# Expert layer of a diffusion trunk: rounds of a fixed mix in its first half, and small experts' rows collected by transfers inside SBUF

## The chip, the cores and the metric

One core of a Trainium2 chip runs the whole forward pass in one launch. The metric is the device time of that launch in microseconds; less is better. The arithmetic is f32, with matmuls either in f32 or as three f32r products of a high and a low part.

## The reference, cut to what matters

A trunk of two layers over 256 latent tokens and 256 context tokens, D = 1024. The first layer's channel mixer is dense. The second one's is a top-2-of-8 expert SwiGLU on the 256 latent tokens, with D_FF_EXPERT = 3584; it is the part that the change touches.

```python
def moe_swiglu(t, router, wg, wu, wd):
    logits = (t @ router).astype(jnp.float32)
    top_val, top_idx = lax.top_k(logits, TOP_K)
    top_w = jax.nn.softmax(top_val, axis=-1)
    gates = jnp.sum(jax.nn.one_hot(top_idx, N_EXPERTS, dtype=jnp.float32) * top_w[..., None],
                    axis=1).astype(t.dtype)
    out = jnp.zeros_like(t)
    for e in range(N_EXPERTS):
        out = out + gates[:, e:e + 1] * swiglu(t, wg[e], wu[e], wd[e])
    return out
```

Each expert needs its three weight matrices, 8 x 3 x 1024 x 3584 x 4 bytes = 352 MB in all, each byte once.

## The kernel before, in words

Everything up to the router runs first. The router then ranks the experts by their number of tokens (rank r = 0 is the fullest; "expert r" below means the expert of rank r) and gives each rank a fixed capacity (CAPS). Tokens are gathered into slots. A slot group of 128 tokens is a "B" unit, of 64 an "A", of 32 a "C". Rank 0 has a B and an A; rank 1 a B and a C; ranks 2 and 3 three C each, as a pair and a single; ranks 4, 5 and 6 an A each; rank 7 one C.

Each expert is worked through in 84 *steps*; a step uses one block of weights of 512 KB (a `raw` tile, 4 KB a partition). 56 steps are for the two up matrices (`up`, in four groups by columns, the last of them 512 wide instead of 1024), 28 for the down matrix (`down`). A B unit's step is `dense`: ACT and VectorE split the block into a high and a low part (`split_w`, L1159 and L1160), and PE runs three f32r matmuls for each product (`mm3`, L243 to L245). A and C units take the block as it is, in f32 (`few`, `mm_few`, L1281), with the tokens packed: a C unit's block is cut into four column pieces that run side by side in four 32-column strips of PE, so its result lies in four groups of 32 partitions, each for a quarter of the columns (an A unit: two groups of 64).

The steps are put into *rounds* by hand. `drive` runs a round thus: the dense matmuls of the round before, the packed ones of this round, then the splits for the next round are handed to ACT and VectorE, then the loads of blocks up to RAW = 16 ahead, then what has come due (`due`, filled by `after(n, ...)`: transposes of hidden values, scatters). PE's order is exactly this order (`manual_schedule`); the other engines' orders are set by the framework's scheduler. SP issues all weight loads, in step order; each waits until its buffer of the ring `raws` is free. The lists are made by `beside` (two steps of the main stream and a share of the others in each round; the last 32 steps alone, four a round). Main are ranks 1, then 0. The others are `weave(whole(7), whole(2) + whole(3))`, which alternates between whole groups (16, 8 or 28 steps) of rank 7 and of ranks 2 and 3, and then ranks 4, 5 and 6. That makes 92 rounds of 7 or 8 steps (4 at the end); rank 1 is main in rounds 0 to 41, rank 0 in 42 to 83. In the first 42 rounds lie 320 of the 672 steps.

When an expert's last step is done, `take` (L1421, L1422) copies the result from PSUM as a high and a low part (`yB`, `yA`, `yC`). `finish` calls `places`: for each slot group POOL copies its part of the placement matrix `pick` side by side to full width (`pd`, L1437, one buffer) and PE transposes it (L1441). In the rounds after, `scatter` (L1470) multiplies the placement with the result, 256 columns at a time where there is a C unit (four rounds, two token tiles each), 512 otherwise; for a C or A unit these are matmuls on 32 or 64 rows, one pair for each slot group. VectorE adds them, times the gate, to `acc` (L1474). The last finished expert (rank 6) takes a way of its own (`fin`, `Final`).

PSUM of the layer: three banks "b" for experts with a B unit, three "a" for the others, two "q" for transposes and scatters.

Of the kernel before, what the change touches and what calls it, by code (L numbers as in the profile page):

```python
# [11 lines left out]
F32R = mybir.dt.float32r  # L12
# [6 lines left out]
D = 1024  # L19
# [26 lines left out]
WIDE = {"B": 128, "A": 64, "C": 32}  # L46


RAW = 16

UPS = [(0, 1024), (1024, 1024), (2048, 1024), (3072, 512)]

# [2 lines left out]
def trunk(ctx: ExitStack, tc: tile.TileContext, I, out, dbg=None):  # L55
    nc = tc.nc
    V, S, G, PE = nc.vector, nc.scalar, nc.gpsimd, nc.tensor
# [36 lines left out]
    def chain(*gens):  # L94
        for g in gens:
            yield from g

    def fr(ap):
        return ap.bitcast(F32)
# [9 lines left out]
    identr = kq.tile([128, 128], F32R, name="identr")  # L109
# [321 lines left out]
    def evac(dst, src):  # L431
        evac_n[0] += 1
        if evac_n[0] % 2:
            S.activation(dst, src, AF.Copy)
        else:
            V.tensor_copy(dst, src)
# [523 lines left out]
    for i in range(DEPTH):  # L960
        last = i == DEPTH - 1
        n = 1 if last else 2
        u = new_u()
# [5 lines left out]
        with ExitStack() as mx:  # L969
            def pools(name):  # L970
                return mx.enter_context(tc.tile_pool(name=f"{name}{i}", bufs=1))

            y = mixer(i, u, n, pools, begun if i == 0 else None, ((filters(), 18),) if i == 0 else (),
                      () if last else ((ada_cols(i, 3), AP + 1),
                                       (chain(ada_cols(i, 4, R_GF), ada_part(i, 2)), 2 * AP + 1)))
# [11 lines left out]
        if not last:  # L987
            u = new_u()
# [16 lines left out]
    i = DEPTH - 1  # L1005
    u = new_u()
# [10 lines left out]
    with tc.tile_pool(name="route", bufs=1) as rp:  # L1017
# [105 lines left out]
        pick = mr.tile([128, 2, 768], F32R, name="pick")  # L1123
        for c0, r, b, kind in COLS:
            w = WIDE[kind]
# [14 lines left out]
    pm = ctx.enter_context(ExitStack())  # L1140
    rawp = pm.enter_context(tc.tile_pool(name="raws", bufs=RAW))
    mp = pm.enter_context(tc.tile_pool(name="moe", bufs=1))
    mps = pm.enter_context(tc.tile_pool(name="mps", bufs=4, space=PSUM))

    def mbank(tag, dt=F32):

        return mps.tile([128, 512], dt, name="m" + tag, tag=tag, bufs={"b": 3, "a": 3, "q": 2}[tag])
# [26 lines left out]
    units = {r: [] for r in range(NE)}  # L1174
    for c0, r, _, kind in COLS:
        u = units[r]
# [12 lines left out]
    def after(n, fn, *args):  # L1189
        due.setdefault(now[0] + n, []).append((fn, args))  # L1190

    def drive(rounds):
        flat = [(n, s) for n, rnd in enumerate(rounds) for s in rnd]
        raws, tiles, ahead = {}, {}, [0, 0]

        def load(upto):
            while ahead[0] < min(upto, len(flat)):
                raws[ahead[0]] = load_raw(flat[ahead[0]][1][1](), *flat[ahead[0]][1][2])
                ahead[0] += 1

        def split(rnd):
            while ahead[1] < len(flat) and flat[ahead[1]][0] <= rnd:
                s = flat[ahead[1]][1]
                load(ahead[1] + 1)
                raw = raws.pop(ahead[1])
                tiles[ahead[1]] = (raw,) + (split_w(raw, *s[2]) if s[3] else ())
                ahead[1] += 1

        load(RAW)
        first_tokens()  # L1210
        split(0)
        n = 0
        with tc.manual_schedule(engines={mybir.EngineType.PE}):
            old = []
            for r, rnd in enumerate(rounds):
                for s, t in old:
                    s[3](t)
                old = [(s, tiles[n + i]) for i, s in enumerate(rnd) if s[3]]
                for i, s in enumerate(rnd):
                    if s[4]:  # L1220
                        s[4](tiles[n + i])
                    tiles.pop(n + i)
                n += len(rnd)
                split(r + 1)
                load(n + RAW)
                for fn, args in due.pop(now[0], []):
                    fn(*args)
                now[0] += 1
                if r == len(rounds) - 3:
                    places(rnd[-1][0])  # L1230
                    fin.append(Final())
            while due:
                now[0] = min(due)
                for fn, args in due.pop(now[0]):
                    fn(*args)

    def beside(main, others, tail):

        out, j, n = [], 0, len(main) // 2
        for i in range(n):  # L1240
            upto = (i + 1) * (len(others) - tail) // n
            out.append(main[2 * i:2 * i + 2] + others[j:upto])
            j = upto
        while j < len(others):
            out.append(others[j:j + 4])
            j += 4
        return out

    def weave(*streams):

        out, done = [], [0] * len(streams)
        total = [sum(map(len, g)) * (1 if i else 0.8) for i, g in enumerate(streams)]
        while any(streams):
            j = min((done[j] / total[j], j) for j in range(len(streams)) if streams[j])[1]
            g = streams[j].pop(0)
            done[j] += len(g)
            out += g
        return out

    def gather(c0, n, dst):  # L1260

# [146 lines left out]
    ys = {}  # L1408

    def take(u, o):  # L1410

        ys[u] = []
        n = min(512, 8 * WIDE[u[0]] * (len(u) - 1))
        for ob in o:
            tag = "big" if u[0] == "B" else "yA" if n == 512 else "yC"
            y = mp.tile([128, 2, n], F32R, name="y" + u[0], tag=tag, bufs=1 if tag == "yA" else 2)
            src = ob[:, 0:n]
            if fin:
                src = mp.tile([128, n], F32, name="yg", tag="sgA", bufs=3)
                V.tensor_mul(src, ob[:, 0:n], fin[0].gy)  # L1420
            S.activation(y[:, 0], src, AF.Copy)  # L1421
            V.tensor_sub(y[:, 1], src, fr(y[:, 0]))  # L1422
            ys[u].append(y)

    pts = {}

    def places(r):

        for u in units[r]:
            w = WIDE[u[0]]  # L1430
            for j, c0 in enumerate(u[1:]):
                if u[0] == "B":
                    pds = [pick[:, t, c0:c0 + 128] for t in range(2)]
                else:
                    g = 128 // w
                    pd = mp.tile([128, 2, g, w], F32R, name="pd", tag="pt")
                    G.tensor_copy(pd, fr(pick[:, :, None, c0:c0 + w]).to_broadcast([128, 2, g, w]))  # L1437
                    pds = [pd[:, t].rearrange("p a s -> p (a s)") for t in range(2)]
                q = mbank("q", F32R)
                for t in range(2):  # L1440
                    PE.transpose(q[:, 128 * t:128 * t + 128], pds[t], identr)  # L1441
                p = mp.tile([128, 2, 128], F32R, name="pt" + u[0], tag="ptF", bufs=6)
                evac(p, fr(q[:, 0:256]).rearrange("p (t s) -> p t s", s=128))
                pts[u, j] = p

    def finish(r):
        if not fin:
            places(r)
        n = 256 if any(u[0] == "C" for u in units[r]) else 512
        cells = [(c0, t) for c0 in range(0, D, n) for t in range(2)]  # L1450
        for j, (c0, t) in enumerate(sorted(cells, key=lambda x: x[1]) if fin else cells):
            after(1 + j // 2, scatter, r, t, c0, n)

    fin = []

    def scatter(r, t, c0, n):
        o = mbank("q")[:, 0:n]
        ops = []
        for u in units[r]:
            w = WIDE[u[0]]  # L1460
            for j in range(len(u) - 1):
                for a in range(2):
                    if u[0] == "B":
                        ops.append((pts[u, j][:, t], ys[u][c0 // 512][:, a, c0 % 512:c0 % 512 + n]))
                    else:
                        q, i = divmod(c0, 8 * w)
                        i += 8 * w * j
                        ops.append((pts[u, j][w * q:w * q + w, t], ys[u][0][w * q:w * q + w, a, i:i + n]))
        for j, (l, m) in enumerate(ops):
            PE.matmul(o, l, m, start=(j == 0), stop=(j == len(ops) - 1))  # L1470
        sl = acc[0][:, t, c0:c0 + n]
        g = gates_r[:, t, r:r + 1]
        if not fin:
            V.scalar_tensor_tensor(sl, o, g, sl, op0=OP.mult, op1=OP.add)  # L1474
        else:
            with tc.issue_after(newest[0].ins):
                sl = fin[0].o[t][:, c0:c0 + n]
                V.scalar_tensor_tensor(sl, o, g, sl, op0=OP.mult, op1=OP.add)
                fin[0].add(t, c0 // 512)

    def whole(r):

        return [g for fb in range(len(UPS)) for g in up(r, fb)] + down(r)

    def flat(groups):
        return [s for g in groups for s in g]
# [33 lines left out]
    def first_tokens():  # L1520
# [5 lines left out]
        for r in range(NE):  # L1526
            for u in units[r]:
# [2 lines left out]
        acc.append(hp.tile([128, 2, D], F32, name="acc", tag="H1"))  # L1530
        G.memset(acc[0], 0.0)

    drive(beside(flat(whole(1) + whole(0)), weave(whole(7), whole(2) + whole(3)) + flat(whole(4) + whole(5) + whole(6)),
                 32))


    flag = nc.values_load(ctli[0:1, 8:9], min_val=0, max_val=NE)
# [128 lines left out]
```

## Time and profile before

| | us |
|---|---|
| runs of the kernel before (median of 3) | 1880.66 |
| their lowest and highest | 1878.2, 1880.77 |
| the profiled execution: its time | 1878.78 |
| the profiled execution: its span | 1877.0 |

The profiled execution is one of the kind of the three; its span is the time from the first to the last instruction. The expert layer's rounds begin at 943.6 us; the last scatter of the layer ends at 1864.6. The engines: PE = TensorE's matmuls, PEld its weight loads, DVE = VectorE, ACT = ScalarE, POOL = GpSimd, SP = SyncE, which issues the weight loads. Ends of matmuls are modelled, so that starts are the better measure of pace: a row's pitch is the distance between two starts. f32 matmuls and their weights are two instructions each. PEclk is the granted clock of TensorE as a share of its full 2.4 GHz; in a short stretch a mean between 0.5 and 1 is a part of it at the lower level.

### The profile page before, as it was taken

The page shows a single profiled execution, that of the slowest core. Times are in us where ns is not written, and L with a number is a line of the kernel's source. Part 1 is how long each engine was busy: PE and PEld are TensorE (multiplying, and loading weights), DVE is VectorE, ACT ScalarE, POOL GpSimd, SP SyncE. Part 2 cuts the span into 40 slices and gives each one's busy share as a digit, 9 for nine tenths or more (in the row PEclk, how much of TensorE's full clock was granted, in tenths as well). Part 3 has the DMA queues.
Part 4 walks back from the last instruction along what each step waited for, and adds up shares of the span by engine and source line. Part 5 has one row for each costly group of instructions (what it writes and reads, how often), then busy time and mean ns, then how long its engine had stood idle before and what let it go on. Part 6 is the DMA issues. An engine that isn't in the chain of part 4 may idle for free.

```text
span 1877.0 us, 34065 instructions
## 1 busy us (share of the span) xinstructions
PE 1792.9 (96%) x13502; PEld 1221.3 (65%) x13502; DVE 896.7 (48%) x1504; ACT 625.3 (33%) x1037; POOL 70.1 (4%) x83
## 2 busy tenths in 40 slices
PE   6999999899999998989799999999999999999996
PEld 3778667778888887987666666667555444454442
DVE  3767764766755556687623323323332333333332
ACT  3554542433223324555432322222322222222221
POOL 0200200000000000010000000000000000000002
PEclk8999999899999999999899999999999999999998
DMA  8233234444545553230599999999997999999995
GB/s 319 87 113 113 90 104 133 147 159 148 190 148 164 171 174 103 79 113 20 182 409 408 376 405 372 382 343 376 399 391 269 367 401 406 378 401 408 393 403 226
DMA packets 193630, 481.91 MB, mean 257 GB/s; under 512 B 16911, under 2 KB 59824, under 8 KB 193335
## 3 DMA queue, kind: packets, MB, share of 16 engines
q1 hardware_dynamic: 187929, 471.68, 68.7%
q10 hardware_dynamic: 5246, 6.94, 1.1%
q8 instruction: 108, 1.77, 0.4%
q0 software_dynamic: 288, 1.05, 0.2%
q14 instruction: 59, 0.48, 0.1%
HBM read 474.36 MB, written 5.24 MB: 256 GB/s over the span
## 4 chain that ended last, share of the span: by engine, by line
PE 84%; DMA 5%; DVE 4%; issue 3%; ACT 2%; POOL 1%; SPq 0%; POOLq 0%; DVEq 0%; ACTq 0%
PE ma L1281 24%; PE psa L243 7%; PE psa L245 7%; PE psa L244 7%; PE mb L1281 6%; PE mb L243 4%; PE mb L245 4%; PE mb L244 4%; PE mq L1470 2%; DMA raw<-in_moe_wd_dram 2%; DMA raw<-in_w_ada_dram 2%; PE mq L1349 1%; PE pss L244 1%; PE pss L245 1%; PE pss L243 1%
## 5 line engine op out<-in xcount | busy, mean ns | idle before, releaser
L1160 DVE TENSOR_TENSOR wlo<-raw,whi 128x1024 fp32r<-128x1024 f32 x168 | 205.6, 1225 | 300.0 <-ACT whi L1159 292.4
L1281 PE MATMUL ma<-raw,xF 128*32 128x256 f32 (+3 forms) x4352 | 326.3, 385 | 5.4 <-issue 5.3
L1159 ACT ACTIVATE whi<-raw 128x1024 fp32r<-128x1024 f32 x168 | 178.0, 1060 | 409.0 <-PE mb L245 406.1
L1281 PEld LDWEIGHTS ma<-raw,xF 128*32 128x32 f32 (+1 forms) x4352 | 167.2, 115 | 154.2 <-issue 77.3
L235 ACT ACTIVATE whi<-raw 128x1024 fp32r<-128x1024 f32 x120 | 125.3, 1045 | 273.3 <-PE pst L245 79.5
L236 DVE TENSOR_TENSOR wlo<-raw,whi 128x1024 fp32r<-128x1024 f32 x120 | 144.8, 1207 | 117.9 <-ACT whi L235 117.7
L243 PE MATMUL psa<-uh,whi 128*128 128x512 f32 (+1 forms) x448 | 174.5, 391 | 0.8 <-DVE uh L386 0.8
L245 PE MATMUL psa<-uh,wlo 128*128 128x512 f32 (+1 forms) x448 | 172.2, 386 | 1.7 <-DVE wlo L236 1.7
L244 PE MATMUL psa<-ul,whi 128*128 128x512 f32 (+1 forms) x448 | 172.4, 385 | 0.0
L1281 PE MATMUL ma<-raw,hF 128*32 128x256 f32 (+1 forms) x1904 | 164.5, 418 | 3.2 <-DMA raw<-in_moe_wd_dram 3.1
L1281 PEld LDWEIGHTS ma<-raw,hF 128*32 128x32 f32 (+1 forms) x1904 | 74.1, 115 | 86.1 <-issue 41.8
L313 DVE SCALAR_TENSOR_TENSOR acc<-raw,cst,acc 128x512 f32<-128x512 f32 x140 | 98.4, 747 | 32.0 <-DMA raw<-in_w_ada_dram 28.0
L245 PEld LDWEIGHTS psa<-uh,wlo 128*128 128x128 f32 x448 | 85.9, 192 | 20.1 <-DVE wlo L236 4.3
L243 PEld LDWEIGHTS psa<-uh,whi 128*128 128x128 f32 x448 | 86.4, 193 | 19.2 <-issue 1.9
L244 PEld LDWEIGHTS psa<-ul,whi 128*128 128x128 f32 x448 | 86.1, 192 | 15.9 <-issue 0.2
L243 PE MATMUL psa<-whi,uh 128*128 128x256 f32 (+1 forms) x288 | 89.6, 312 | 5.7 <-DVE t L424 3.2
L243 PE MATMUL mb<-whi,xB 128*128 128x512 f32 x224 | 94.9, 424 | 0.0
L245 PE MATMUL mb<-whi,xB 128*128 128x512 f32 x224 | 89.2, 398 | 0.0
L244 PE MATMUL mb<-wlo,xB 128*128 128x512 f32 x224 | 89.1, 398 | 0.0
L244 PE MATMUL psa<-wlo,uh 128*128 128x256 f32 (+1 forms) x288 | 88.4, 307 | 0.7 <-DVE wlo L236 0.7
L245 PE MATMUL psa<-whi,ul 128*128 128x256 f32 (+1 forms) x288 | 87.9, 307 | 0.0
L1281 PE MATMUL mb<-raw,xF 128*32 128x256 f32 (+3 forms) x768 | 84.3, 422 | 0.0
(388 smaller groups left out, 2686.6 us busy)
## 6 DMA issues: line engine op xcount, KB each, us to landing
raw<-in_moe_wg_dram SPq DMA_DIRECT2D x224, 512.0 KB, 8.3
raw<-in_moe_wu_dram SPq DMA_DIRECT2D x224, 512.0 KB, 7.7
raw<-in_moe_wd_dram SPq DMA_DIRECT2D x224, 512.0 KB, 9.0
raw<-in_w_ada_dram SPq DMA_DIRECT2D x112, 256.0 KB, 3.9
raw<-in_w_ada_dram SPq DMA_DIRECT2D x40, 512.0 KB, 5.4
raw<-in_w_in_dram SPq DMA_DIRECT2D x36, 512.0 KB, 4.5
raw<-in_ffn_wg_dram SPq DMA_DIRECT2D x22, 512.0 KB, 4.1
raw<-in_ffn_wu_dram SPq DMA_DIRECT2D x22, 512.0 KB, 3.8
```

The lines of the kernel that those rows point to most:

```text
L235: S.activation(hi, raw, AF.Copy)
L236: V.tensor_sub(lo, raw, fr(hi))
L243: PE.matmul(ps, l[0], r[0], start=first, stop=False)
L244: PE.matmul(ps, l[0], r[1], start=False, stop=False)
L245: PE.matmul(ps, l[1], r[0], start=False, stop=last)
L313: V.scalar_tensor_tensor(a[:, sl], raw, c, a[:, sl], op0=OP.mult, op1=OP.add)
L1159: S.activation(hi, raw, AF.Copy)
L1160: newest[0] = V.tensor_sub(lo, raw, fr(hi))
L1281: PE.matmul(o[s * h:s * h + s, n * j:n * j + n], x, w[:, n * h:n * h + n], start=first and j == 0, stop=last, tile_position=(0, s * h), sk ...
L1349: PE.transpose(q[:, 128 * c:128 * c + 128], s[:, 128 * c:128 * c + 128], ident)
L1470: PE.matmul(o, l, m, start=(j == 0), stop=(j == len(ops) - 1))
```

## The change

Three things are changed, all in the expert layer.

- The order of steps in the first 42 rounds. `weave` goes; `even` makes rounds of 2 steps of rank 1, 4 of ranks 2 and then 3, and 2 of rank 7. The second half is `beside` with rank 0 as the main stream and ranks 4, 5, 6 as the others. In the first 42 rounds now lie 336 steps; there are 92 rounds as before.
- The way of the results of ranks 2, 3, 4 and 5 (`direct` tells the others) from `take` to `scatter`. `together` clears a tile `z` of 128 partitions x 2 x 512 (POOL) and POOL issues transfers from SBUF to SBUF that put the slot groups' results, for one half of the columns, under each other: for ranks 2 and 3 six of 64 KB for each half, for 4 and 5 one of 256 KB. Three rounds later `scatter` multiplies `z` with one full placement of 128 slots (made by two transposes, without POOL's copy), 512 columns at a time; then the second half's transfers are issued, and three rounds later it is scattered.
- Buffers: RAW 15 instead of 16, one of 4 KB for `z`, `yC` three instead of two, placements (`ptF`) four instead of six.

```diff
-RAW = 16
+LAST = 6
+RAW = 15
...
-    def weave(*streams):
...
+    def even(main, *others):
+
+        n = len(main) // 2
+        return [main[2 * i:2 * i + 2] + [s for o in others for s in o[len(o) // n * i:len(o) // n * (i + 1)]]
+                for i in range(n)]
...
-            y = mp.tile([128, 2, n], F32R, name="y" + u[0], tag=tag, bufs=1 if tag == "yA" else 2)
+            y = mp.tile([128, 2, n], F32R, name="y" + u[0], tag=tag, bufs={"big": 2, "yA": 1, "yC": 3}[tag])
...
+    def turned(pds):
+        q = mbank("q", F32R)
+        for t in range(2):
+            PE.transpose(q[:, 128 * t:128 * t + 128], pds[t], identr)
+        p = mp.tile([128, 2, 128], F32R, name="ptF", tag="ptF", bufs=4)
+        evac(p, fr(q[:, 0:256]).rearrange("p (t s) -> p t s", s=128))
+        return p
+
+    def direct(r, u):
+
+        return u[0] == "B" or r in (0, 1, 7, LAST)
+
     def places(r):
...
+            elif direct(r, u):
...
     def finish(r):
         if not fin:
             places(r)
-        n = 256 if any(u[0] == "C" for u in units[r]) else 512
-        cells = [(c0, t) for c0 in range(0, D, n) for t in range(2)]
-        for j, (c0, t) in enumerate(sorted(cells, key=lambda x: x[1]) if fin else cells):
-            after(1 + j // 2, scatter, r, t, c0, n)
+        near = [u for u in units[r] if direct(r, u)]
+        far = [(u, j, c0) for u in units[r] if not direct(r, u) for j, c0 in enumerate(u[1:])]
+        if near:
...
+                after(1 + j // 2, scatter, r, t, c0, n, near)
+        if far:
+            first = min(far[0][2], 640)
+            pts["far", r] = turned([pick[:, t, first:first + 128] for t in range(2)])
+            together(r, 0, far, first)
+            for hb in range(2):
+                if hb:
+                    after(3, together, r, 1, far, first)
+                for t in range(2):
+                    after(3 + 3 * hb, scatter, r, t, 512 * hb, 512, ["far"])
+
+    zs = {}
+
+    def together(r, hb, far, c0):
+
+
+        z = mp.tile([128, 2, 512], F32R, name="z", tag="z", bufs=1)
+        G.memset(fr(z), 0.0)
+        for u, j, c in far:
+            w = WIDE[u[0]]
+            n = 8 * w
+            for i in range(512 // n):
+                q = 512 // n * hb + i
+                G.dma_start(fr(z[c - c0:c - c0 + w, :, n * i:n * i + n]), fr(ys[u][0][w * q:w * q + w, :, n * j:n * j + n]))
+        zs[r] = z
...
-    def scatter(r, t, c0, n):
+    def scatter(r, t, c0, n, parts):
         o = mbank("q")[:, 0:n]
         ops = []
...
+                if u == "far":
+                    ops.append((pts[u, r][:, t], zs[r][:, a]))
...
-    drive(beside(flat(whole(1) + whole(0)), weave(whole(7), whole(2) + whole(3)) + flat(whole(4) + whole(5) + whole(6)),
-                 32))
+    drive(even(flat(whole(1)), flat(whole(2) + whole(3)), flat(whole(7)))
+          + beside(flat(whole(0)), flat(whole(4) + whole(5) + whole(6)), 32))
```

## Rows read from the trace of the kernel before

**Rows 1.** The page: what the transfers moved in 40 equal slices, GB/s.
```profile
GB/s 319 87 113 113 90 104 133 147 159 148 190 148 164 171 174 103 79 113 20 182 409 408 376 405 372 382 343 376 399 391 269 367 401 406 378 401 408 393 403 226
```

**Rows 2.** Windows: stretch, length, PE PEld DVE ACT POOL busy, PEclk, DMA share, GB/s.
```profile
943.60:1373.70 430.10, 419.51 (x6146) 275.07 (x6145) 135.74 (x164) 114.64 (x154) 3.41 (x5) 1.00 1.01 386
1373.70:1864.60 490.90, 485.75 (x2605) 237.94 (x2604) 158.79 (x186) 119.94 (x151) 14.46 (x14) 0.99 0.97 374
1335.00:1350.00 15.00, 11.78 (x107) 6.04 (x100) 4.02 (x6) 3.19 (x5) 0.40 (x1) 0.89 1.03 408
1344.00:1352.00 8.00, 6.64 (x42) 3.84 (x46) 0.74 (x2) 1.84 (x4) 0.40 (x1) 0.79 1.03 408
1416.00:1424.00 8.00, 6.85 (x26) 4.35 (x28) 2.67 (x5) 2.50 (x3) 1.21 (x3) 0.79 0.36 144
1444.00:1451.00 7.00, 7.00 (x30) 5.17 (x31) 2.67 (x4) 1.72 (x2) 0.00 (x0) 0.76 0.87 347
```

**Rows 3.** PE's waits from 900 us on: total, times, longest.
```profile
PE ma L1281 <- issue: 5.3, 3, 2.1
...
PE ma L1281 <- DMA raw<-in_moe_wd_dram: 3.1, 5, 0.8
```

**Rows 4.** The weight queue's own waits from 900 us on, the two longest.
```profile
SPq L1151 <- DVE wlo L1160: 301.3, 123, 8.1
SPq L1151 <- PE ma L1281: 112.6, 276, 3.3
```

**Rows 5.** The chain that ended last, in order of time: start, length, what.
```profile
930.48 7.88 DMA raw<-in_moe_wg_dram
...
963.80 7.77 PE ma L1281 x144
...
1169.84 2.59 PE ma L1281 x48
...
1294.78 2.12 issue
...
1326.03 10.33 DMA raw<-in_moe_wd_dram
1336.48 10.12 DMA raw<-in_moe_wd_dram
...
1437.37 5.15 PE ma L1281 x24
```

**Rows 6.** Timeline of PE: two dense steps, then two packed ones of expert 0.
```profile
1402.31 0.50 PE L243 MATMUL mb<-whi,xB 128*128 128x512 f32 x1
...
1405.25 1.94 PE L1281 MATMUL mb<-raw,xF 128*64 128x512 f32 x8
```

**Rows 7.** Timeline of PE at expert 2's end: placements, then two scatters.
```profile
1155.92 0.37 PE L1441 MATMUL mq<-identr,pd 128*128 128x128 f32 x2
...
1157.83 0.36 PE L1441 MATMUL mq<-identr,pd 128*128 128x128 f32 x2 [0.59 <-POOL pd L1437]
...
1164.17 1.69 PE L1470 MATMUL mq<-yC,ptC 32*128 32x256 f32 x12
1165.79 0.50 PE L243 MATMUL mb<-whi,xB 128*128 128x512 f32 x1
```

**Rows 8.** Timeline of PE: two scatters of expert 4, and the next start.
```profile
1589.11 1.49 PE L1470 MATMUL mq<-yA,ptA 64*128 64x512 f32 x4
1590.52 0.50 PE L243 MATMUL mb<-whi,xB 128*128 128x512 f32 x1
```

**Rows 9.** The tile hfs, loaded through POOL's queue: issue (ns) and landing.
```profile
L751 POOL DMA_DIRECT2D hfs<-hf x2: 608/704/799, 178.5 to 828.9; - x2
...
DMA to landing us min/median/max: 3.8/3.9/4.0
```

**Rows 10.** Timeline of POOL: the first placement copy, and the clear of acc.
```profile
931.23 0.40 POOL L1437 CAST pd<-pick 128x256 fp32r<-128x256 f32 x1 [21.15 <-DVE pick L1127]
943.77 1.80 POOL L1531 MEMSET acc<- 128x2048 f32 x1 [12.14 <-PE mb L1267]
```

More of the change, by code (lines that the diff above doesn't have):

```diff
@@ L1247, in beside @@
         return out
-    def weave(*streams):
[L1251 to L1258, printed above, removed]
+    def even(main, *others):
+        n = len(main) // 2
+        return [main[2 * i:2 * i + 2] + [s for o in others for s in o[len(o) // n * i:len(o) // n * (i + 1)]]
+                for i in range(n)]
     def gather(c0, n, dst):
@@ L1425, in trunk @@
     pts = {}
+    def turned(pds):
[7 more added lines that the diff above has]
+        return u[0] == "B" or r in (0, 1, 7, LAST)
     def places(r):
         for u in units[r]:
[L1430 to L1444, printed above, removed]
+            if u[0] == "B":
+                pts[u] = turned([pick[:, t, u[1]:u[1] + 128] for t in range(2)])
+            elif direct(r, u):
+                w = WIDE[u[0]]
+                pd = mp.tile([128, 2, 128 // w, w], F32R, name="pd", tag="pt")
+                G.tensor_copy(pd, fr(pick[:, :, None, u[1]:u[1] + w]).to_broadcast([128, 2, 128 // w, w]))
+                pts[u] = turned([pd[:, t].rearrange("p a s -> p (a s)") for t in range(2)])
     def finish(r):
@@ L1448, in finish @@
             places(r)
-        n = 256 if any(u[0] == "C" for u in units[r]) else 512
-        cells = [(c0, t) for c0 in range(0, D, n) for t in range(2)]
-        for j, (c0, t) in enumerate(sorted(cells, key=lambda x: x[1]) if fin else cells):
-            after(1 + j // 2, scatter, r, t, c0, n)
+        near = [u for u in units[r] if direct(r, u)]
+        far = [(u, j, c0) for u in units[r] if not direct(r, u) for j, c0 in enumerate(u[1:])]
+        if near:
+            n = 256 if any(u[0] == "C" for u in near) else 512
+            cells = [(c0, t) for c0 in range(0, D, n) for t in range(2)]
+            for j, (c0, t) in enumerate(sorted(cells, key=lambda x: x[1]) if fin else cells):
+                after(1 + j // 2, scatter, r, t, c0, n, near)
@@ new lines, in finish @@
+        if far:
[12 more added lines that the diff above has]
+        for u, j, c in far:
+            w = WIDE[u[0]]
+            n = 8 * w
[3 more added lines that the diff above has]
+        zs[r] = z
@@ L1454, in trunk @@
     fin = []
-    def scatter(r, t, c0, n):
+    def scatter(r, t, c0, n, parts):
         o = mbank("q")[:, 0:n]
         ops = []
[L1459 to L1468, printed above, removed]
+        for u in parts:
+            for a in range(2):
+                if u == "far":
+                    ops.append((pts[u, r][:, t], zs[r][:, a]))
+                elif u[0] == "B":
+                    ops.append((pts[u][:, t], ys[u][c0 // 512][:, a, c0 % 512:c0 % 512 + n]))
+                else:
+                    w = WIDE[u[0]]
+                    q, i = divmod(c0, 8 * w)
+                    ops.append((pts[u][w * q:w * q + w, t], ys[u][0][w * q:w * q + w, a, i:i + n]))
```

## The prediction

> **What bounds the kernel now.** I read the slices first: from slice 20 on, the expert layer, the transfers run near 400 GB/s with two dips, to 343 and 269 [rows 1]. That looks like a layer bound by its transfers. The windows say otherwise: over rounds 0 to 41 (943.6 to 1373.7 us) and from round 42 to the last scatter (to 1864.6), PE is busy 419.5 of 430.1 us and 485.8 of 490.9 us, the transfers move 386 and 374 GB/s, and in a window where nothing holds them back they move 408 [rows 2]. So both are nearly full, and the waits decide who waits for whom. In the whole layer PE waits 3.1 us for the weights, in five waits, and 5.3 us for nothing that the profile shows ("issue") [rows 3]. The queue that issues the weight loads waits 301 us for the split of an earlier block and 113 us for a matmul [rows 4]: it waits until PE gives a buffer back. PE's order is the bound; the weights arrive ahead of it, except in one place.
>
> That place shows in the chain of waits. One step (one 512 KB block) of experts 2 and 3 costs PE 7.77 / 6 = 1.30 us, one of expert 7 2.59 / 6 = 0.43 us, one of experts 4 to 6 5.15 / 6 = 0.86 us [rows 5]; two dense steps cost 1405.25 - 1402.31 = 2.94 us, and a 64-column packed step of expert 0 1.94 / 2 = 0.97 us at most [rows 6]. At 408 GB/s a block of 524,288 bytes takes 1.29 us; the chain's transfer pieces of 10.33 and 10.12 us are about eight of them each [rows 5]. A round of two expert-1 steps (2.94 dense, 2 x 0.43 packed) and six of expert 2 costs PE 3.80 + 7.77 = 11.6 us against 10.3 of transfer; with six of expert 7 it costs 6.4 us. The old weave puts all 28 down steps of expert 7 into rounds 35 to 39, some 39 blocks, 50 us of transfer, for about 32 us of PE. There the buffers run empty: the chain goes over to the transfers [rows 5], and between 1335 and 1350 us PE is busy 11.8 of 15 us at a granted clock of 0.89 [rows 2].
>
> **The change part by part.** The sum is made against the profiled execution (span 1877.0, its run 1878.8; the median of the runs shown is 1880.7).
>
> *Even rounds.* A round of the first half becomes 2 steps of expert 1, 4 of 2 or 3, 2 of 7: PE 2.94 + 0.86 + 4 x 1.30 + 0.86 = 9.9 us, with some 0.3 us of transposes about 10.2; the transfer of its 8 blocks 8 x 1.29 = 10.3. Nearly level, with the transfers 0.1 us a round behind, over 42 rounds some 5 us. The loads start before PE does (a block is in flight by 930.5 us [rows 5], PE's rounds start at 943.6), which is a lead of some 13 us; so I expect the lead to shrink to about 8 and no wait for weights to be left. The second half becomes 2 + 5.24 blocks a round instead of 2 + 5.6: PE 2.94 + 2 x 0.93 + 5.24 x 0.86 = 9.3 against 9.35 of transfer, level again, with the scatters on top of PE. The number of steps is the same, so the gain is not the balance itself but what the imbalance cost. (a) The wait for expert 7's blocks: PE's row has 3.1 us [rows 3], the records' ends are modelled, eight such matmuls being shown at 0.64 where their pitch is 0.43 us, so up to 5; I take 4.5. (b) The clock after it: 8 us at 0.79 granted [rows 2], one stretch at the lower of the two levels, 8 x 0.21 = 1.7 us. (c) "Issue": 5.3 us in three waits, all where experts 2 and 3 work on their 512-wide blocks, whose steps hold twice the matmuls (a 2.12 us piece in the chain [rows 5]). These steps now come 4 a round beside others instead of 4 or 5, so most of it may stay: I take 2 away, with 0 and 5.3 as ends.
>
> *One buffer fewer (15).* In the second half a load is issued when PE frees a slot, and PE hardly waits, so the ring is longer than it needs there. I cost it at nothing; what hides it is the lead of about 13 us. If the lead were gone, it would cost up to the 1.29 us of one block each time the ring ran dry.
>
> *Experts 2 and 3 collected.* Now expert 2's end costs PE three transposed copies of the placement with a POOL cast between them, 1155.92 to 1158.19 = 2.3 us (the first and the last of three shown), and four rounds of two scatters, each 1165.79 - 1164.17 = 1.62 us: 6.5 us [rows 7]; together 8.8. After, there is one pair of transposes without a cast, at most 0.37 us as the first one here, and four cells of two 128-row, 512-column matmuls. The trace has no such cell for this line's packed kind, the nearest is expert 4's, 64 rows and 512 columns, two cells in 1590.52 - 1589.11 = 1.41 us [rows 8]; the number of columns is the same, so 4 x 0.70 = 2.8. Together 3.2: 5.6 us less for each of the two experts, 11.2 in sum, all on PE's own path, which has no gaps to hide it.
>
> *Experts 4 and 5 collected.* Four cells of two 512-column matmuls before and after; only a POOL cast that nobody waits for goes. Zero.
>
> *The transfers and POOL.* Experts 2 and 3 add 12 transfers of 64 KB each, 4 and 5 add 2 of 256 KB each: 2.6 MB, at 408 GB/s 6.4 us of the engines that carry the weights, in four places, under a lead of 8 us or more: nothing. Each collection is a clear of 4 KB a partition (half of the 1.80 us clear of acc, 0.9 us [rows 10]), then up to six issues at 0.6 to 0.8 us, then a landing; the only two issues of POOL in the trace landed in 3.8 to 4.0 us, at 512 KB [rows 9]. That is 0.9 + 6 x 0.8 + 4 = 10 us after the rows are cut, and PE asks for them three rounds, about 30 us, later: hidden, with 20 us to spare. Queued behind the waiting issues on POOL are the second collection and expert 1's cast; expert 7's cast is not, since POOL takes the first cast as soon as its data is there (at 931.23, two hundred us before its use at 1155.92 [rows 7, 10]). Expert 1's cast is wanted a round after, later than those 10 us. Below nothing this cannot go; above, it is the first rival.
>
> The page "SBUF — State Buffer" of the Trainium skill (section "SBUF: two separate sides") speaks against moving this to POOL: it says that descriptors of a POOL transfer can't be written while VectorE runs a copy that takes both ports, and gives 0.62 us growing to 3.1 us. No run here shows that yet; the two POOL transfers above landed in 3.9 us. If each of six issues grew by that 2.5 us, an estimate from that page, a collection would take 25 us instead of 10, still inside the 30.
>
> *The clock at the half.* Around 1418 and 1445 us the granted clock falls for two short stretches, 8 us at 0.79 and 7 at 0.76 [rows 2], 1.7 + 1.7 us, in rounds in which expert 3's cast-bound transposes and 32-row scatters stand between the dense steps. Half of those go, those of experts 7 and 1 now fall into the same rounds: I take 1.5 away, ends 0 and 3.4.
>
> *New waits.* Experts 2 or 3 (two PSUM banks) and 7 (one) hold all three banks of their ring from now on, and three experts end at rounds 41 and 42: +1, ends 0 and 8.
>
> Sum: -11.2 - 4.5 - 1.7 - 2 - 1.5 + 1 = -19.9. Span 1857.1, 1858.9 from the profiled run, 1860.8 from the median; I say 1859.
>
> **The rivals.** *Slower: the full bank ring.* When experts 2/3 or 7 begin a new group, their first matmul needs a bank that ACT or VectorE has just emptied. If the emptying is queued behind the next round's split (which itself waits for PE's dense step), PE stands until about 2 us into it. There are 18 such changes for experts 2 and 3 and 9 for expert 7, most at the same rounds. At 1.5 us each over 27 it costs 40 us: 1900. It beats the gain from 0.75 us a change on. Against it: among PE's waits now, no row names the two lines that empty these banks, though with two of three banks held a new group's second bank had to be emptied within 1.3 us; and now 4 to 5 us of other work (expert 7's two steps, the dense pair) lies between. *The rows come late.* If a collection took over 30 us, PE would stand in eight places; at 32.5 us each that is 20 us and the gain is gone: 1879. For it: POOL has issued two transfers in the whole trace, never beside a full weight queue; against it the 20 us to spare. *The first half is bound by its transfers.* If eight blocks come at 10.5 us instead of 10.3, the lead of 13 us is used up by round 40 and some 5 to 8 us of waits for weights and a slow stretch of the clock come in its place: 1867. *Everything goes.* No issue wait, no slow stretch, no new wait: -11.2 - 5 - 1.7 - 5.3 - 3.4 = -26.6: 1852.
>
> **How the numbers follow.** Forecast (1854 to 1864) 0.58; everything goes 0.13; bound by transfers or part of the new waits (1864 to 1872) 0.14; rows late, about no change, 0.06; full ring, slower, 0.09. The range takes in the third and the second case: the best bounds give 1852 less 2 for cheaper cells (their matmuls are full-height), the worst 1859 + 12; 1850 to 1871 leaves out the last two. 0.2% of the time is 3.8 us, about what a measurement here can tell from no change. Faster: 0.58 + 0.13 + 0.14 = 0.85; same 0.06; slower 0.09.
>
> **What would show it.** PE's waits for moe_wd blocks gone and the clock at 1.00 through the first half; expert 2's and 3's scatters four cells at about 0.7 us with no wait for a transfer before them; the round starts about 10.2 us apart; the dip in the slice around 1420 us smaller. Wrong would be: waits of PE named after ACT's or VectorE's emptying of the ma banks at every fourth round, waits named after z, or waits for moe_w blocks before round 42.

## The result, and the profile after

The changed kernel took 1861.55 us (median of 4 runs, 1858.17 to 1862.95); the kernel before, run beside it, 1879.8 (1878.2 to 1880.77). The ratio is 0.9899, with a 95% interval from 0.9887 to 0.9912: 18 us faster, where the sum had 20. The profiled execution, the fastest of the four, took 1858.17 us; its span is 1856.4, against 1857.1 in the sum. That agreement of the total is partly luck: the experiments below show that the parts don't add up in the way in which the sum added them.

The slices of the page of after, what the transfers moved and the granted clock:

```profile
GB/s 319 91 114 104 90 114 127 129 161 151 177 169 171 170 152 136 80 93 45 109 387 408 404 399 407 376 403 403 402 387 378 372 394 401 399 390 394 402 404 227
PEclk8999999899999999999899999999999999999998
```

Of the two dips [rows 1], the one to 343 is gone (403), and where 269 stood there is now 378; the lowest slice left is the next one, 372. The windows of after, with the columns of [rows 2]: the rounds 0 to 41, the rounds from 42 to the last scatter, the place of expert 7's old down steps, and the place of the dip:

```profile
945.70:1380.20 434.50, 431.00 (x6479) 281.55 (x6478) 134.03 (x157) 114.86 (x154) 10.15 (x15) 1.00 1.03 401
1380.20:1843.90 463.70, 458.69 (x2185) 220.94 (x2183) 158.40 (x183) 119.17 (x150) 26.35 (x31) 0.99 1.00 383
1344.00:1352.00 8.00, 8.00 (x121) 5.10 (x114) 1.56 (x2) 0.74 (x3) 0.00 (x0) 1.00 1.02 407
1416.00:1424.00 8.00, 8.00 (x37) 4.26 (x38) 4.11 (x5) 2.72 (x3) 2.16 (x5) 1.00 1.03 322
```

The first half moves 401 GB/s instead of 386 and holds 336 blocks instead of 320 in 434.5 us instead of 430.1: 1.293 us a block instead of 1.344. PE is at full clock in it. PE's waits in the layer (total, times, longest), and the two longest of the weight queue:

```profile
PE mq L1499 <- DVE acc L1503: 1.2, 4, 0.4
PE ma L1279 <- issue: 1.1, 1, 1.1
PE mq L1347 <- issue: 0.9, 1, 0.9
...
PE ma L1279 <- DMA raw<-in_moe_wg_dram: 0.2, 1, 0.2
...
SPq L1154 <- DVE wlo L1163: 269.6, 120, 5.6
SPq L1154 <- PE ma L1279: 100.0, 247, 3.3
```

No wait for a moe_wd block is left and none is named after `z`; "issue" has fallen from 5.3 to 2.0 us [rows 3]; the weight queue still waits mostly for buffers, but 32 us less for the splits than in [rows 4].

The end of expert 2 on PE's timeline of after (start, length, line, operation): its two transposes, and the two pairs of cells, three and six rounds later:

```profile
1160.17 0.36 PE L1428 MATMUL mq<-identr,pick 128*128 128x128 f32 x2
1160.37 0.46 PE L246 MATMUL mb<-whi,xB 128*128 128x512 f32 x1
...
1190.45 1.21 PE L1499 MATMUL mq<-z,ptF 128*128 128x512 f32 x4
1191.49 0.39 PE L246 MATMUL mb<-whi,xB 128*128 128x512 f32 x1
...
1223.55 1.20 PE L1499 MATMUL mq<-z,ptF 128*128 128x512 f32 x4
1225.13 0.33 PE L1347 MATMUL mq<-ident,sg 128*128 128x128 f32 x1 [0.37 <-DVE acc L1503]
```

From start to start that is 0.20 + 1.04 + 1.58 = 2.8 us, against 8.8 as the prediction read [rows 7] (8.6 from start to start). The tile `z` of after (issue time in ns, then the landing):

```profile
L1480 POOL DMA_DIRECT2D z<-yC x24: 533/534/631, 1161.0 to 1417.6; - x24
L1474 POOL MEMSET z<- x8: 951/955/956, 932.5 to 1741.9; 128x1024 f32 x8
...
DMA to landing us min/median/max: 5.3/6.9/7.6
```

Six issues take 3.2 us, the landing up to 7.6: from the first issue to the last landing some 10 us, with the clear ahead of them 11. The estimate was 10 with the clear; the landing is slower than in [rows 9] and the issues are quicker.

### The profile page after: what moved, and what is told of

Same layout as the page of the kernel before. It is cut to its first block, busy times and chain, and to the rows that moved or that the text cites. A ratio compares the mean times of both kernels' runs of the same rounds, so it can differ in the third digit from the quotient of the medians.

```text
span 1856.4 us, 33972 instructions
## 1 busy us (share of the span) xinstructions
PE 1780.3 (96%) x13414; PEld 1214.3 (65%) x13414; DVE 895.2 (48%) x1494; ACT 624.7 (34%) x1035; POOL 89.5 (5%) x111
## 3 DMA queue, kind: packets, MB, share of 16 engines
q8 instruction: 107, 1.75, 0.4%
## 4 chain that ended last, share of the span: by engine, by line
PE 86%; DVE 5%; issue 3%; DMA 3%; ACT 2%; POOL 1%; SPq 0%; POOLq 0%; DVEq 0%; ACTq 0%
PE ma L1279 25%; PE psa L246 8%; PE psa L248 8%; PE psa L247 7%; PE mb L1279 6%; PE mb L246 5%; PE mb L248 4%; PE mb L247 4%; PE mq L1499 1%; PE mq L1347 1%; PE pss L247 1%; PE pss L246 1%; PE pss L248 1%; PE psa L726 1%; PE psa L264 1%
## 5 line engine op out<-in xcount | busy, mean ns | idle before, releaser
L248 PEld LDWEIGHTS psa<-uh,wlo 128*128 128x128 f32 x448 | 85.9, 192 | 19.9 <-DVE wlo L239 4.0
```

The lines of the kernel that those rows point to most:

```text
L248: PE.matmul(ps, l[1], r[0], start=False, stop=last)
```

## The experiments

The two parts of the change were run alone first, then single sizes and places. Beside the medians I give the mean granted clock around the half, since that turned out to be where the kernels differ; (1 - clock) x length is the time that it can have cost at most.

**Even rounds alone.** The rounds of after, with the results of all experts multiplied directly, as before. The 15 buffers and the third `yC` come along.

```diff
-    drive(beside(flat(whole(1) + whole(0)), weave(whole(7), whole(2) + whole(3)) + flat(whole(4) + whole(5) + whole(6)), 32))
+    drive(even(flat(whole(1)), flat(whole(2) + whole(3)), flat(whole(7)))
+          + beside(flat(whole(0)), flat(whole(4) + whole(5) + whole(6)), 32))
```

> The kernel before with the new order of steps alone (and what it needs: 15 buffers, a third yC); experts 2 to 5 are scattered directly as before. My theory (the two parts add up, PE is the bound, and the order gives back only what the uneven rounds cost): PE's rounds end 8 to 11 us earlier than before, some 1869 to 1872 us, no wait for moe_wd blocks, clock 1.00 around 1344 us, the 11 us of the long scatters still there. Rival (the order is the main gain, through the level load of the transfers): 1862 or less. Rival (the order gives nothing by itself): 1878 to 1880.

Measured: 1886.79 us (1884.29 to 1889.08), ratio 1.0040, 1.0026 to 1.0054: slower than the kernel before (1879.56 beside it), where my theory had it 8 to 11 us faster. PE's timeline of this kernel, at the start of rounds 42 to 46 and at what stands ahead of three of them:

```profile
1393.46 0.36 PE L1436 MATMUL mq<-identr,pd 128*128 128x128 f32 x2 [0.59 <-POOL pd L1432]
1393.66 0.64 PE L243 MATMUL mb<-whi,stB 128*128 128x512 f32 x1
...
1408.01 0.76 PE L243 MATMUL mb<-whi,xB 128*128 128x512 f32 x1
...
1418.40 2.05 PE L1465 MATMUL mq<-yC,ptC 32*128 32x256 f32 x14
1420.66 0.49 PE L1465 MATMUL mq<-yC,ptC 32*128 32x256 f32 x2 [0.21 <-DVE acc L1469]
...
1423.98 0.80 PE L243 MATMUL mb<-whi,xB 128*128 128x512 f32 x1
...
1440.14 0.80 PE L243 MATMUL mb<-whi,xB 128*128 128x512 f32 x1
...
1456.35 0.80 PE L243 MATMUL mb<-whi,xB 128*128 128x512 f32 x1
...
1461.77 2.06 PE L1276 MATMUL mb<-raw,xF 128*64 128x512 f32 x8
```

and its windows over these rounds, and over two of the dense pairs in them:

```profile
1393.00:1462.00 69.00, 67.29 (x268) 39.61 (x270) 24.01 (x36) 13.19 (x17) 1.21 (x3) 0.80 0.70 255
1438.00:1445.00 7.00, 7.00 (x19) 5.22 (x18) 1.98 (x4) 1.06 (x1) 0.00 (x0) 0.51 0.48 195
1455.00:1462.00 7.00, 7.00 (x19) 4.89 (x20) 2.19 (x3) 1.78 (x3) 0.00 (x0) 0.52 0.52 206
```

The last dense pair takes 1461.77 - 1456.35 = 5.42 us instead of 2.94 [rows 6]: it runs at the lower level, 1.2 GHz, throughout. PE is shown busy 67.3 of the 69 us, and the weights come at 255 GB/s. At 0.80 the clock costs up to 13.8 us here. No row of PE's waits in this run names a weight block, so the buffer fewer is not the cause. The four rounds between these starts take 62.7 us. In after they take 48.5:

```profile
1380.24 0.47 PE L246 MATMUL mb<-whi,stB 128*128 128x512 f32 x1
...
1401.66 0.50 PE L1499 MATMUL mq<-yB,ptF 128*128 128x256 f32 x2 [0.34 <-DVE acc L1503]
...
1428.78 0.69 PE L246 MATMUL mb<-whi,xB 128*128 128x512 f32 x1
...
1433.33 1.94 PE L1279 MATMUL mb<-raw,xF 128*64 128x512 f32 x8
```

So 14 us of the 29 between the two profiles (spans 1885.8 and 1856.4) lie in these four rounds; 13.4 are there by the start of round 42 (1393.66 against 1380.24), some 6 of them expert 2's direct way. Even rounds alone bring the gain at expert 7's old place (from 1344 to 1352 us PE is busy 8.0 of 8.0 us at 1.00) and lose more than that at the half.

**Collection alone.** The old weave, with the new way of the results and the 15 buffers.

```diff
-    drive(even(flat(whole(1)), flat(whole(2) + whole(3)), flat(whole(7)))
-          + beside(flat(whole(0)), flat(whole(4) + whole(5) + whole(6)), 32))
+    drive(beside(flat(whole(1) + whole(0)), weave(whole(7), whole(2) + whole(3)) + flat(whole(4) + whole(5) + whole(6)), 32))
```

> The changed kernel with the old order of steps (the weave), so the collection alone, with its 15 buffers. My theory: 11 to 12 us less from the scatters of experts 2 and 3, but the hole of the transfers in rounds 38 and 39 stays, or deepens by the PE time saved before it (some 3 us): 1868 to 1872 us. Rival (the parts do not add up, the collection frees the whole gain): 1862. Rival (without level rounds its time is lost again in the hole): 1876 to 1880.

Measured: 1870.57 us (1869.45 to 1871.09), ratio 0.9955 (0.9938 to 0.9971), 9.0 us less than before: as expected. Its waits of PE in the layer, a window where they stand, and the half:

```profile
PE ma L1284 <- DMA raw<-in_moe_wd_dram: 4.0, 7, 0.7
PE ma L1284 <- issue: 2.5, 2, 1.8
PE mb L246 <- issue: 2.3, 1, 2.3
...
PE ma L1284 <- DMA raw<-in_moe_wu_dram: 1.6, 3, 0.7
...
PE ma L1284 <- DMA raw<-in_moe_wg_dram: 0.7, 1, 0.7
...
1305.00:1314.00 9.00, 6.74 (x98) 5.49 (x88) 0.83 (x3) 1.34 (x2) 0.00 (x0) 0.81 1.03 410
1392.00:1460.00 68.00, 67.65 (x504) 34.84 (x503) 21.02 (x27) 13.52 (x16) 7.27 (x13) 1.00 0.95 336
```

The buffers run empty at expert 7's bunches as in [rows 3], for 6.3 us instead of 3.1, and the clock falls beside it; those are what the even rounds take away. At the half the clock is at 1.00 throughout in this profile: with the old weave, collecting expert 3 removes both stretches of [rows 2].

The two parts alone are worth +7.2 and -9.0 us, together -18.2: some 16 us belong to neither, only to the pair. The profiles show where most of them lie. At the half the clock costs up to 3.4 us before, nothing with the collection alone, 13.8 with the even rounds alone and 1.7 with both: if the parts added up it would be 10.4, so 8.7 belong to the pair (5.3 by the repeat of the changed kernel below, where it costs 5.1). By the waits for weight blocks (3.1, 6.3, none and 0.2) another 3 do, 2 by the repeat. The rest, 5 to 9 us, I can't assign; the buffer fewer, which both runs carry and which is so counted twice, may have a part in it.

**The even rounds, with expert 7's 16 direct matmuls five rounds later.** If the loss of the first experiment came from three experts ending together, moving the cheapest of them away had to give much of it back, though nothing is removed.

```diff
-            after(1 + j // 2, scatter, r, t, c0, n)
+            after((6 if r == 7 else 1) + j // 2, scatter, r, t, c0, n)
```

> The even rounds alone with direct scatters (the run that came out slower than before) and expert 7's scatters moved from rounds 42 to 45 to rounds 47 to 50. My theory (even rounds end experts 3, 7 and 1 together, and the loss is their direct scatters in the same rounds: slow stretches of the clock in rounds 42 to 46, 9 us in that run, and bank waits of 4 us): at least half of it comes back, 1876 to 1881 us, with fewer slow stretches. Rival (expert 3's 48 matmuls of 32 rows beside expert 1's do it, expert 7's 16 don't matter): 1884 to 1888 us.

Measured: 1879.24 us (1872.12 to 1880.42), ratio 0.9997 (0.9984 to 1.0009): 7.5 less than the even rounds alone, as expected. The window over the same rounds is at 0.92 instead of 0.80:

```profile
1392.00:1460.00 68.00, 67.44 (x303) 37.24 (x302) 22.72 (x31) 15.78 (x20) 0.80 (x2) 0.92 0.83 300
```

That is 8.4 us less by the clock (13.8 less 5.4), about the whole difference. Expert 1's scatter cells fall from 9.3 to 7.0 us, expert 7's from 4.6 to 3.5.

**The same move in the changed kernel.** Expert 7's direct matmuls in rounds 47 to 50.

```diff
-                after(1 + j // 2, scatter, r, t, c0, n, near)
+                after((6 if r == 7 else 1) + j // 2, scatter, r, t, c0, n, near)
```

> The changed kernel with expert 7's direct scatters moved from rounds 42 to 45 to rounds 47 to 50; nothing else. My theory (it is the coincidence with expert 1's scatters that makes the q-bank waits and the slow stretch): 1.5 to 3 us less, 1858.5 to 1860 us. Rival (only the number of such matmuls counts, not their neighbours): the same as the changed kernel, 1861.5 us.

Measured: 1859.11 us (1858.79 to 1862.36), ratio 0.9898 (0.9882 to 0.9913). No stretch of lower clock is left around the half (1.00 from 1380 to 1440 us, against 0.97 in after, where the pair at 1428.78 takes 4.55 us). The 2.4 us are as many as expected, but lie within the spread of after's own runs.

**All small experts but the last collected,** 1 and 7 too, from rounds 47 and 51, with two rounds instead of three between asking and use.

```diff
-        return u[0] == "B" or r in (0, 1, 7, LAST)
+        return u[0] == "B" or r in (0, LAST)
...
+    LATER = {1: 5, 7: 10}
```

> The changed kernel with the small units of experts 7 and 1 collected as well, one expert after another (1 from round 47, 7 from round 51), so that rounds 42 to 46 hold only four 128-row cells of expert 1 and the collected ones of expert 3. My theory (direct scatters of 32-row matmuls of several experts in the same rounds cost PE their own time, waits for the q banks and stretches of the lower clock): expert 7's scatter 4.3 to 2.3 us, expert 1's 6.9 to 4.6, the stretch around 1430 us gone (1.6), 1.5 us of bank waits gone: 6 to 7 us less than the changed kernel, 1854 to 1856 us. Rival (the stretches come from elsewhere, the collection's transfers or expert 0's start): 1857 to 1862 us with a slow stretch still in rounds 42 to 46.

Measured: 1856.98 us (1854.39 to 1861.58), ratio 0.9888 (0.9869 to 0.9906): 4.6 us less than the changed kernel, where 6 to 7 were expected. The edit collects and moves later at once, so it can't tell the one from the other. The rounds around the half of this kernel:

```profile
1380.00:1440.00 60.00, 59.24 (x284) 27.61 (x278) 22.60 (x25) 18.36 (x24) 7.27 (x13) 1.00 1.03 386
```

Full clock, and PE busy 59.2 of 60 us. To set it against the changed kernel, both were run again on one chip, with the kernel before for the spread of its front part:

> The kernel that collects experts 7 and 1 as well, once more, beside the changed kernel on the same chip. My theory: 4 to 6 us less than the changed kernel; rival: its 4.6 us in separate calls were the spread of the part ahead of the expert layer, and they are level within 2 us.

> The changed kernel once more, beside the next run on the same chip: 1858 to 1863 us.

> The kernel before once more, to see how far the start of its rounds (943.6 us in the first profile) moves without any change: by up to 3 us if the later starts of the other kernels are the spread of the part ahead of the layer; rival: it stays within 0.5 us, and the later starts come from the new order of the first splits.

Measured: 1858.25 (1855.68 to 1859.52) for collecting all, ratio 0.9883 (0.9869 to 0.9898), and 1861.45 (1859.84 to 1862.35) for the changed kernel, 0.9901 (0.9887 to 0.9916). The runs of the two on this chip don't overlap, the intervals of their ratios do, and 3.2 us, less than the 4 to 6 expected, are 0.17%: it is the fastest kernel of the study, by about what the comparison can just tell. The kernel before took 1881.11; its rounds started at 945.3 us instead of 943.6, so that the start moves by 2 us with no change to the code. In this second profile of collecting all there is one wait for a block in round 42, and the clock falls right behind it:

```profile
1391.70 1.08 PE L1279 MATMUL ma<-raw,xF 128*64 128x512 f32 x4 [1.72 <-DMA raw<-in_moe_wg_dram]
...
1393.00:1397.00 4.00, 4.00 (x12) 3.17 (x12) 0.65 (x2) 1.06 (x1) 0.00 (x0) 0.57 1.03 406
```

**Twelve buffers instead of 15.**

```diff
-RAW = 15
+RAW = 12
```

> The changed kernel with 12 weight buffers instead of 15. My theory (PE is the bound, blocks lie some 10 us or more before they are used): three blocks less take 3.9 us from that lead, the time stays within 0 to 4 us of the changed kernel, 1861 to 1866. Rival (the first half is now bound by its transfers, the lead is used up): each bunch of steps makes PE wait, 1872 or more, with waits for moe_w blocks in the first half.

Measured: 1866.22 us (1865.76 to 1867.6), ratio 0.9936 (0.9919 to 0.9952), 4.7 more than after, a little above the 0 to 4 expected. Its waits for blocks, and its one window of lower clock around the half:

```profile
PE ma L1279 <- DMA raw<-in_moe_wg_dram: 3.3, 4, 1.8
...
1420.00:1427.00 7.00, 7.00 (x18) 5.02 (x18) 2.20 (x4) 1.06 (x1) 2.52 (x5) 0.52 0.84 277
```

The waits stand where the lead is least, in rounds 24 and 42, the longest at 1392 us. Three buffers are 3.9 us of transfer (3 x 1.29), and they are missed. So the lead at the half was thinner than I thought; the next section follows it.

**The rows asked for one round later instead of three.**

```diff
-                    after(3, together, r, 1, far, first)
+                    after(1, together, r, 1, far, first)
...
-                    after(3 + 3 * hb, scatter, r, t, 512 * hb, 512, ["far"])
+                    after(1 + hb, scatter, r, t, 512 * hb, 512, ["far"])
```

> The changed kernel with the collected rows asked for one round after their transfers are issued instead of three. By my estimate a collection takes about 10 us and a round 10 us, so the three rounds hide it three times over: 0 to 5 us more than the changed kernel (at most a wait of 1 to 2 us in the second halves of experts 2 and 3, whose clear comes first), 1861 to 1866. Rival (POOL's transfers come late, 20 us and more, beside the weights): PE waits 8 times for 10 us, 1940.

Measured: 1868.08 us (1864.73 to 1875.05), ratio 0.9937 (0.992 to 0.9954), 6.5 more than after: more than expected, and far from the rival's 1940. PE's wait for `z`, one of its three places, and the window behind it:

```profile
PE mq L1499 <- DMA z<-yC: 3.4, 3, 1.4
...
1395.04 1.17 PE L1499 MATMUL mq<-z,ptF 128*128 128x512 f32 x4 [0.96 <-DMA z<-yC]
...
1397.00:1404.00 7.00, 6.59 (x19) 4.86 (x18) 2.54 (x5) 1.45 (x2) 3.80 (x8) 0.51 1.03 358
```

A round of 10 us and a collection of 10 us are level, so PE waits three times for 3.4 us in all; the clock behind the wait shown costs up to another 7 x 0.49 = 3.4, and two more such stretches follow at 1414 and 1441. Two rounds were enough for the smaller collections of experts 1 and 7 in the kernel that collects all; for those of 2 and 3 they weren't tried.

**Experts 4 and 5 direct again.**

```diff
-        return u[0] == "B" or r in (0, 1, 7, LAST)
+        return u[0] == "B" or r in (0, 1, 4, 5, 7, LAST)
```

> The changed kernel with experts 4 and 5 scattered directly as before, experts 2 and 3 still collected. My prediction put this part at zero (four cells of the same width either way): the same as the changed kernel, within 1.5 us. Rival (64-row cells cost PE or its clock as the 32-row ones do): 3 us or more slower.

Measured: 1864.91 us (1859.16 to 1868.66), ratio 0.9918 (0.9903 to 0.9934). 3.5 more than the changed kernel on the same chip, which is the rival's number. But the cells of the two experts take 5.2 us from start to start, against 4.1 collected. Between the two profiles lie 5.6 us, and 3.8 of them are there by round 52, ahead of the first place where this edit acts: 1.6 from the start of the rounds on, and 2.2 from round 42 on, where PE waits twice for a block in this profile:

```profile
1392.44 1.94 PE L1279 MATMUL ma<-raw,xF 128*64 128x512 f32 x4 [0.99 <-DMA raw<-in_moe_wg_dram]
...
1392.50:1399.50 7.00, 6.83 (x20) 4.14 (x21) 1.34 (x3) 0.50 (x2) 0.40 (x1) 0.51 1.03 408
```

Its range overlaps after's. By the cells the edit costs about 1 us; a total can't be told from the spread of round 42, and this run is inconclusive.

## Why the prediction was right, and which step was not

The terms, by starts of matmuls in the two profiles, against the sum:

- *Experts 2 and 3 collected*: -11.2 forecast. The two experts' placements and cells took 17.1 us before and 5.6 after (2.6 + 0.2 for each): -11.5. The cell, taken from expert 4's at 0.70, is 0.52 in the first pair above (1.04 / 2) and 0.79 in the second, where VectorE's addition into `acc` has to be waited for. Collection alone, 9.0 us, agrees.
- *The wait for expert 7's blocks and the clock behind it*: -4.5 - 1.7 forecast, -5.9 measured: before, rounds 38 and 39 took 8.2 and 9.4 us, where PE's like work took 6.6 and 6.1 in the rounds ahead, and the dense pair behind was 1.0 us longer. The window 1344 to 1352 is now 8.0 of 8.0 us at 1.00.
- *Issue*: -2 forecast, -3.3 measured.
- *New waits*: +1 forecast. The transposes of hidden values cost 1.5 us more, the cells of experts 7 and 1 0.8: +2.3 in all.
- *The start of the rounds*, not in the sum: 945.7 instead of 943.6, +2.1, which a repeat of the kernel before shows too (945.3). The starts of all the changed kernels lie between 945.5 and 948.8, so that some part of it may belong to the change; this stays open.
- *Experts 4 and 5*: zero forecast; 4.8 us before, 4.1 after: -0.7.
- *The clock at the half*: -1.5 forecast. In this profile one stretch is left of two, -1.7. In the repeat of after there are two, at 1405 and 1419, in other rounds than here and together up to 5.1 us against 3.4 in both profiles of the kernel before, +1.7, and its layer is 4 us longer. The term changes its sign from one profile to the next, so that its agreement here is luck.

With -1.9 us that I can't assign, these make -20.6 in the span; the sum said -19.9.

**The step that failed** is "half of those go, those of experts 7 and 1 now fall into the same rounds: I take 1.5 away". It took the half as a place with two fixed stretches and let the even rounds and the collection act on it in one sum. The experiments show that each changes there what the other is worth. By the lists of steps, expert 7 ended in round 39 before, expert 1 in 41 and expert 3 in 44; level rounds end all three in round 41, and what each leaves falls due in the rounds after. Their casts, transposes and 32-row scatters then stand together between the dense pairs of rounds 42 to 46, and the clock there falls to 0.80 over 69 us, up to 13.8 us against 3.4 in [rows 2]. Collecting expert 3 takes the largest of the three out again (after: 0.97). So even rounds, which the sum credited with some 8 us, cost 7 alone, and the collection, credited with 11, is worth 25 once the rounds are even. For 7.5 of these 15 us that the even rounds fall short by, the coincidence and not the even order as such is shown to be the cause, by the move of expert 7's 16 matmuls with no work taken out. For the rest, experts 1 and 3 side by side, it is argued: they were not moved apart alone.

*What makes the clock fall* is not settled. In three of the profiles shown a wait of PE for a block or for `z`, from 0.96 to 1.72 us, stands right ahead of a stretch at half clock. But the other two waits for `z` of the next-round kernel, 1.38 and 1.04 us in the first half, bring no fall; and with 12 buffers, in the repeat of after and with expert 7's matmuls moved there are waits of 1.75, 1.06 and 1.13 us for a block in the same round 42, and the dense pair behind each is at full clock. In the even rounds alone, waits of 0.59 us for POOL's cast and of 0.21 for a bank whose content VectorE adds to `acc` stand ahead of the stretches; after has a wait of 0.34 us of that kind at 1401.66, and the pair behind it is at full clock. The page "TensorE: Matmul & The Clock Gate" of the Trainium skill (section "A second HAM failure mode: psum-queue depth-cycling") tells of a kernel whose clock swings because PE idles briefly between groups while it cycles through PSUM banks. The trace agrees in so far as waits of 0.21 and 0.22 us for a bank stand ahead of stretches in the even rounds alone; the wait of 0.34 us without a fall speaks against taking it as the whole rule.

**The rivals.** The *full bank ring* did not come: among PE's waits none names the lines that empty the `ma` banks. *Rows late* is out by 20 us of slack, and with two of the three rounds taken away PE waits 3.4 us, not 20. The issues did not grow by 2.5 us: they take 0.53 us each (0.63 at most), with VectorE busy 1.57 of 6 and 2.85 of 7 us in the windows of two collections (last section). The page "SBUF — State Buffer" of the Trainium skill (section "SBUF: two separate sides") lets one expect growth where VectorE runs a copy that takes both ports; the issues show none, and whether it has a part in the longer landing, 7.6 us at most, no run here shows. *The first half bound by its transfers* comes nearest: a plain round takes 10.0 us on PE (10.2 forecast), the mean of the half is 10.3, level with the transfers, and there is one wait of 0.2 us; with 12 buffers there are four, 3.3 us in all.

*The lead* was named but mis-sized. From each block's landing, worked out from the bytes of the weight queue, to its first matmul, the least lead in a round is some 11 us at the start, 9 to 11 until round 20, 7.5 behind the first collection, 5 to 6 behind the second and some 5 in round 42; I had 13 falling to 8. With 12 buffers it is 3 to 4 in the last three of these places. The cost of a collection in lead, which I put at nothing, is a part of the reason; from round 34 to 42 the lead falls by 3 us with no collection under way, by some 0.4 us a round where I had 0.1.

## What to carry to other kernels

Price a reordering by what comes to end together, not only by what runs level: what an expert leaves to do at its end is cheap alone and dear in a heap. Measure the parts of a change alone before adding their gains, even if the total comes out as forecast. Behind a wait of 1 to 2 us the clock was low in three profiles, for up to 3.4 us of cost, and not in three others, so the thinnest point of a lead deserves the buffers.

## What the runs showed of the hardware

I had not expected that six transfers of 64 KB would slow the weights as much as they did. The windows of after without a collection, and around the first two:

```profile
1100.00:1150.00 50.00, 50.00 (x708) 31.32 (x707) 15.29 (x16) 11.94 (x13) 0.00 (x0) 1.00 1.03 407
1164.00:1170.00 6.00, 6.00 (x116) 3.64 (x112) 1.57 (x2) 0.49 (x1) 0.29 (x1) 1.00 1.04 313
1196.00:1203.00 7.00, 7.00 (x129) 4.82 (x122) 2.85 (x5) 0.38 (x1) 0.13 (x1) 1.00 1.05 311
```

Split by queue, the weights move 245 GB/s in the first of these two and the collection 65 (252 and 56 in the second). With 405 otherwise, 6 us x (405 - 245) = 0.96 MB of weights stay behind for 0.39 MB collected: some 2.4 us of lead each, where the bytes alone are worth 1.0. The page "DMA: Bandwidth & Descriptors" of the Trainium skill (section "SWDGE vs HWDGE vs iDMA") says that each engine takes turns between the queues that feed it; the trace agrees in so far as both queues move at once. That does not say why the sum of the two falls to 313 and 311 GB/s: the engines are shown busy all through (DMA share 1.04 and 1.05), and what fills them was not tried.
